# Two small loads on ScalarE's queue and the first token tile on the sync queue, in a one-layer hybrid attention kernel

## The chip, the core and the metric

The kernel runs on one core of one Trainium2 chip. The metric is device time in microseconds (us) of one execution; several executions are timed and the median is taken. Engines are named as in the profile: PE (TensorE; PEld its weight loads), DVE (VectorE), ACT (ScalarE), POOL (GpSimd), SP (the sync engine, which only issues transfers). A transfer can be issued by SP, ACT or POOL; the profile calls their queues SPq, ACTq and POOLq.

## The reference

One layer over 512 tokens of width 2048, float32: a norm, one wide projection, two groups of attention heads, gates, one output projection, a residual.

```python
h = rms_norm(x, norm_g)                      # x 512 x 2048, norm_g 2048
proj = h @ w_in                              # 2048 x 8192: qA kA vA gA | qB kB vB gB, 1024 columns each
ya = stick_breaking_attention(qA, kA, vA)    # 8 heads of 128, strictly causal
yb = chunk_band_attention(qB, kB, vB, q_norm_g, k_norm_g, rel_bias)   # 8 heads, band of 9 chunks of 64
mixed = concat(ya * silu(gA), yb * silu(gB))
out = x + mixed @ w_out                      # 2048 x 2048
```

The factor `norm_g` is applied to the channels of x before the projection; the division by the root mean square is per token and is applied later, to results.

## The kernel before

All products are float32, made of float32r halves: a tile is split into a high part (a copy to float32r, on ACT) and a low part (the difference, on DVE), and a product is three matmuls (high by high, high by low, low by high). Most of the projection goes through Winograd's seven products for a 2 x 2 block matrix. Output columns come in 32 units of 256, and the contraction of 2048 channels in steps.

The token side: the 16 channel blocks of x (128 channels x 512 tokens, 256 KB each, `xT[:, j, :]`) are paired, block j with block j + 8. `activations(j, 0)` loads a pair into one tile of four quarters of 256 columns: its `first` transfer (L687) fills quarters 0 and 3 with block j, its `second` (L688) fills quarters 1 and 2 with block j + 8. Pair 0 and pair 1 lie in the tile `xq`. `raw_split` then makes the high part on ACT with the channel's factor from `ng_t` as scale (L766), and the low part on DVE (L767); for quarter 3 of pair 0 the high part is made on DVE as well (L764).

The weight side: the weights of steps 0 and 1 (`n` below 2, the first two units, rows of the first two pairs) come in eight pieces of 128 KB, `load(n, i, kk)` (L384). `split` makes their high parts on ACT (L454) and their low parts on DVE (L458). The first product of the program needs piece (0, 0, 0), the `first` half of pair 0 and `ng_t`. The first two units use wide products only: each is one matmul at L773 and two at L775, of 512 columns. Eight matmuls on zeros (L1573) run ahead of them.

`ng_t` is a tile of 128 x 16 (64 bytes per partition, 8 KB), the whole of `norm_g`. In the kernel before it is loaded by POOL, with `pool.dma_start(ng_t, ng)` (L130), ahead of POOL's constants (L1574 to L1578). ACT issues one transfer in all, the `first` of pair 0, ahead of loading its function table (L1582). Every other load of this part is issued by SP.

What sets the order on each engine is a planner inside the kernel. Generators (`step_weights`, `activations`, `split`, and so on) yield operations `Op(engine, cost, fn, due)`; the planner keeps a clock of its own, and on each engine takes the operation with the earliest due time among those that are ready. `need(k, before)` is a due time: the moment at which product k begins by the planner's table, less `before`. So a different queue or due time at the start can also change, by a few rows, what the planner does later. A transfer's landing is told by one of eight semaphores for ACT's and SP's queues together (`DMAHW0` to `DMAHW7` in the listings below), given out in turn; the ninth transfer waits until the one that had its semaphore has landed. POOL's transfers have others (`DMASW`).

After the statistics of x (`x_stats`, `x_rstd`), DVE makes four diagonal blocks (L1233) and PE multiplies them by ones (L1240), which spreads the tokens' factors over the partitions. This stands where the Winograd products of the later units (L846 and L848) begin.

Of the kernel before, what the change touches and what calls it, by code (L numbers as in the profile page):

```python
# [15 lines left out]
P = 128  # L16
# [14 lines left out]
H = 256  # L31
# [43 lines left out]
def trunk_kernel(ctx: ExitStack, tc: tile.TileContext, xT, xn, wi, wqk, wo, ng, qg, kg, rel, out):  # L75
# [29 lines left out]
    act, dve, pe, sp, pool = nc.scalar, nc.vector, nc.tensor, nc.sync, nc.gpsimd  # L105

    def single(shape, name, dt=F32):
        return cp.tile(shape, dt, tag=name, name=name)

    def tmp(shape, tag, name, dt=F32, bufs=1):  # L110
        return wp.tile(shape, dt, tag=tag, name=name, bufs=bufs)

    ident = single([P, P], "ident")
    ng_t = single([P, NK], "ng_t")
# [12 lines left out]
    halves = banks.rearrange("p a (b c) -> p (a b) c", c=H)  # L127
    mixd = [dp.tile([P, S], F32, tag=f"mixd{i}", name=f"mixd{i}") for i in range(2 * NG)]

    pool.dma_start(ng_t, ng)  # L130

    KB = 256
    arena = single([P, 28 * KB], "arena")
# [8 lines left out]
    def avail(r):  # L142

        return all(r[1] <= x[0] or x[1] <= r[0] for x in taken.values())

    def claim(key, r):
        assert avail(r), (key, r, taken)
        taken[key] = r
        return arena[:, r[0]:r[1]] if r[0] < 100 * KB else parts[:, r[0] - 100 * KB:r[1] - 100 * KB]
# [39 lines left out]
    def AC(w, fn, due=None, n=1):  # L189
        return Op("ACT", (0.085 + 0.85e-3 * w) * n, fn, due)  # L190
# [14 lines left out]
    def advance(gen, rank):  # L205
        r = next(gen, None)
        if r is None:
            return
        if isinstance(r, Op):

            wait = 0.06 if r.engine != "PE" else 1.4 if position[0] < at_step[step_of[NU-4, 0]] else 0.6
            later(clock[0] + wait, lambda: ready[r.engine].append((r, gen, rank, count[0])))
        else:
            waiting.append((rank, r, gen))

    def spawn(gen, rank=(0,)):
        advance(gen, rank)
# [60 lines left out]
    def chunk(u):  # L278
        g, kind = u // 4, u % 4
        return (16 if g % 2 else 0) + kind * 4 + g // 2  # L280
# [4 lines left out]
    def rows(n):  # L285


        u, r = steps_[n]
        if u < NU:
            return (wi[chunk(u), h + r // 2, :, r % 2 * 2:r % 2 * 2 + 2, :] for h in (0, 2))  # L290
        q, i, h = u - NU, r // 2, r % 2
        return (wo[2 * i + k, q, :, h, :].rearrange("p (a b) -> p a b", b=H) for k in (1, 0))
# [9 lines left out]
    def plain(u, r):  # L302
        return u < 2 or u == NU and r < PLAIN_STEPS
# [67 lines left out]
    def need(k, before=0.0):  # L371

        return lambda: clock[0] + begins[k] - begins[position[0]] - before

    wt_, whl, at_end = {}, {}, {}

    def wt_place(n):
        return WT[olds.index(n) % 3]

    def load(n, i, kk=None):  # L380
        if n not in wt_:
            wt_[n] = claim(("wt", n), wt_place(n))
        x = slice(0, 2) if kk is None else slice(kk, kk + 1)
        sp.dma_start(wt_[n][:, 2 * i * H:2 * (i + 1) * H].rearrange("p (a b) -> p a b", b=H)[:, x, :], list(rows(n))[i][:, x, :])  # L384
        if i and kk != 0:
            done.add(("loading", n))

# [5 lines left out]
    def step_weights(n):  # L393
        i_ = olds.index(n)
        yield lambda: n < 2 or ("loading", olds[i_ - 1]) in done
        if n > before_major[-1]:
            yield lambda: ("taken", NM - 1) in done
        yield lambda: avail(wt_place(n))
        k = at_part[n, 0]
        if n < 2:  # L400

            for kk in range(2):
                for i in range(2):
                    k_ = k + 2 * i + 2 * len(BOTH) * kk
                    yield Op("SP", 0.47, lambda: load(n, i, kk), need(k_, 8), lag=P * 1024, quick=True)
                    spawn(landed_half(n, k_, i, kk), (0, n, i))
            return

        def both():
            for i in range(2):  # L410
                load(n, i)

        yield Op("SP", 0.94, both, need(k, 11 if n < 2 * NR else 7), lag=P * 4096)
        if plain(*steps_[n]):
            yield from split(n, 0, k)
        else:
            yield from sums(n, k, at_part[n, 1])

    def landed_half(n, k, i, kk):
        at_ = dma_free[0] + LANDING  # L420
        later(at_, lambda: None)
        yield lambda: clock[0] >= at_ - 1e-9
        yield from split(n, 0, k, i, kk)
# [11 lines left out]
    def split(n, part, k, piece=None, kk=None):  # L435

        w = (8 * P, 6 * P)[part]
        c = slice(0, w) if piece is None else slice(piece * w // 2, (piece + 1) * w // 2)
        if kk is not None:
            c = slice(c.start + kk * H, c.start + (kk + 1) * H)  # L440
        t = wt_[n][:, part * 8 * P + c.start:part * 8 * P + c.stop]
        i = having[part].index(n)
        yield lambda: i < 1 or ("hi", having[part][i - 1], part) in done
        yield lambda: n < before_major[-1] + 1 or ("hl", NP * NM - 1) in done
        homes = WHL[part] + ([(116 * KB, 124 * KB)] if n < 2 * NR else [])
        yield lambda: (n, part) in whl or any(avail(x) for x in homes)

        def hi():
            if (n, part) not in whl:
                r_ = next(x for x in homes if avail(x))  # L450
                whl[n, part] = claim(("w", n, part), r_).rearrange("p (a b) -> p a b", a=2)
                at_end.setdefault(last_use[n, part], []).append(("w", n, part))
                done.add(("hi", n, part))
            act.copy(whl[n, part][:, 0, c], t)  # L454

        yield AC(c.stop - c.start, hi, need(k, 2.6))
        h, l = whl[n, part][:, 0, :], whl[n, part][:, 1, :]
        yield DV(c.stop - c.start, lambda: dve.tensor_tensor(out=l[:, c], in0=t, in1=h[:, c].bitcast(F32), op=ALU.subtract),  # L458
                 need(k, 0.5))
        for x in (2,) if part else (0, 1) if piece is None else (piece,):  # L460
            done.add(("w", n, x) if kk is None else ("w", n, x, kk))
        if part or all(("w", n, x) in done or all(("w", n, x, y) in done for y in range(2)) for x in range(2)):
            done.add(("split", n, part))
            if ("split", n, 0) in done and (("split", n, 1) in done or (n, 1) not in at_part):
                unclaim(("wt", n))
# [187 lines left out]
    def activations(j, mixed):  # L653

        if mixed:
# [4 lines left out]
            k = at_step[step_of[NU, j]]  # L660
            kt, dt = at_step[step_of[NU + plain(NU, j), j]], 0
        else:
            k = at_step[step_of[0, j // 2]] + (2 * len(BOTH) if j == 1 else 0)
# [7 lines left out]
        if mixed:  # L671
            if HOME[j] == "qk" and "qk" not in staged:
                staged["qk"] = tmp([P, 2, 4 * H], "qk", "xm")
            r = staged["qk"][:, 0, :] if HOME[j] == "qk" else tmp([P, 4 * H], HOME[j], f"x{j}{mixed}")
        elif STAGE[j % 6] == "qk":
            if "x" not in staged:
                staged["x"] = tmp([P, 2, 4 * H], "qk", "xq")
            r = staged["x"][:, j % 2, :]
        else:
            r = tmp([P, 4 * H], STAGE[j % 6], f"x{j}")  # L680
# [2 lines left out]
        f = lambda x: x.rearrange("p a b -> p (a b)")  # L683
        a, b = (mixd[NJ + j], mixd[j]) if mixed else (xT[:, j, :], xT[:, j + NJ, :])

        queue, engine = (act, "ACT") if j == 0 and not mixed else (sp, "SP")
        first = lambda: queue.dma_start(r.rearrange("p (a b) -> p a b", b=H)[:, 0:4:3, :], a.rearrange("p (a b) -> p a b", b=H))  # L687
        second = lambda: sp.dma_start(r[:, H:3 * H], b)  # L688
        one = ("B11",), f(h[:, :1]), f(l[:, :1])
        spawn(raw(j, mixed, Op(engine, 0.47, first, need(k, 10 if mixed or j != 1 else 9), lag=P * 2048), r, k,  # L690
                  [(0, 1) + one] + ([(3, 4, ("B12",)) + ((f(h[:, 6:]), f(l[:, 6:])) if not mixed else (None, None))] if not mixed or plain(NU, j) else []), j, not mixed, kt, dt), (0, 0, j))
        spawn(raw(j, mixed, Op("SP", 0.47, second, need(k + 2 * mixed, 7.95 if engine == "ACT" else 9), lag=P * 2048), r, k + 2,
                  [(1, 3, ("B21", "B22"), f(h[:, 1:3]), f(l[:, 1:3]))], j + NJ, not mixed, kt, dt), (0, 0, j))
        yield lambda: all(("scaled", j, i, mixed) in done for i in (j, j + NJ))
        if mixed:
# [45 lines left out]
    def raw(j, mixed, load_, r, k, parts, channels, scaled, kt, dt):  # L741
        yield load_
        g_ = ng_t[:, channels:channels + 1] if scaled else None
        for x in parts:
            spawn(raw_split(j, mixed, r, k + 3 if mixed and x[2] == ("B12",) else k, g_, *x), (0, 0, j))
        if scaled and parts[-1][2] == ("B12",):

            yield lambda: ("x", j, "B12", 0) in done and position[0] >= START
            s_ = r[:, 3 * H:]
            yield AC(H, lambda: act.activation(s_, s_, AF.Copy, scale=g_), need(kt, 6 + dt))  # L750
        done.add(("scaled", j, channels, mixed))
# [41 lines left out]
    for k in reversed(range(len(program))):  # L793
        n, x, a = program[k]
        u = steps_[n][0]
        b = major_bank(*steps_[n]) if major(u) else place(u, a, x[2]) // 2
# [812 lines left out]
    for g in range(NG):  # L1609
        for h in range(2):  # L1610
            n = head(g, h)
# [52 lines left out]
```

## Time and profile before

| what | value |
|---|---|
| median of 3 runs | 906.84 us (906.5 to 908.52) |
| the profiled execution's own time | 908.72 us |
| its span, first to last instruction | 907.0 us, so 1.72 us lie outside it |
| PE busy | 898.4 us, 99% |
| DVE busy | 768.6 us, 85% |
| ACT busy | 636.8 us, 70% |
| POOL busy | 67.9 us, 7% |
| transfers on ACT's queue | 1, of 256 KB, 3.7 us from issue to landing |
| load of `ng_t` on POOL's queue | 8 KB, 4.1 us from issue to landing |

In a timeline row stand the start, the time from there to the end of the last instruction of the row, the engine, the line, the operation and its count; in brackets the engine's idle time before it and what ended that. In a row of transfers stand the queue, the count, the size of one and the median time from issue to landing. A row of windows has the stretch, its length, and for each engine its busy time and instructions, then the granted clock, the busy share of the transfer engines and GB/s.

### The profile page before, as it was taken

To read this page: it belongs to the slowest core of one execution; us is meant where nothing else is said; L and a number is where in the kernel's file an instruction comes from. 1 tells how busy PE (TensorE), PEld (TensorE's weight loads), DVE (VectorE), ACT (ScalarE), POOL (GpSimd) and SP (SyncE) were. 2 spreads that over 40 slices of the span, in tenths; PEclk is the share of its full clock that TensorE was granted. 3 is DMA by queue.
4 is the path that set the end of the run, shared out by engine and by line. 5 is a ranking of instruction groups with operands and counts; after the bars stand their busy time and mean duration, and the time that the engine had idled before them with its cause. 6 is when DMAs were issued, how large, how long until landed. Compare 5 with 4: busy or idle time off the path is not lost.

```text
span 907.0 us, 15445 instructions
## 1 busy us (share of the span) xinstructions
PE 898.4 (99%) x5504; PEld 802.1 (88%) x5504; DVE 768.6 (85%) x1255; ACT 636.8 (70%) x1203; POOL 67.9 (7%) x92
## 2 busy tenths in 40 slices
PE   8999999999999999999999999999999999999997
PEld 6898888888888888888888888888888988999997
DVE  6999989788898878788979787889878988988786
ACT  7785967697688658885877588868767885544342
POOL 0001100010000010000000100010000000101011
PEclk9999999999999999999999999999999999999999
DMA  8767677767666877677768775776665536657371
GB/s 303 247 202 170 155 171 182 183 154 177 172 164 154 198 184 168 157 174 184 166 151 207 182 168 142 184 192 159 151 163 126 186 116 206 159 197 190 114 186 47
DMA packets 187725, 156.22 MB, mean 172 GB/s; under 512 B 8944, under 2 KB 157440, under 8 KB 187648
## 3 DMA queue, kind: packets, MB, share of 16 engines
q1 hardware_dynamic: 177552, 122.45, 44.9%
q0 software_dynamic: 9824, 32.52, 22.0%
q8 instruction: 43, 0.70, 0.3%
q14 instruction: 34, 0.28, 0.1%
q10 hardware_dynamic: 272, 0.26, 0.1%
HBM read 117.45 MB, written 8.39 MB: 139 GB/s over the span
## 4 chain that ended last, share of the span: by engine, by line
PE 95%; DMA 2%; DVE 1%; ACT 1%; issue 0%; SPq 0%; DVEq 0%; POOLq 0%
PE banks L846 39%; PE banks L775 20%; PE banks L848 19%; PE banks L773 10%; PE banks L1479 2%; PE banks L836 2%; DMA arena<-in_wi 1%; PE banks L1385 1%; PE banks L837 1%; PE banks L1502 1%; DMA ng_t<-in_ng 0%; DVE parts L576 0%; ACT parts L575 0%; PE banks L1311 0%; DVE co L1074 0%
## 5 line engine op out<-in xcount | busy, mean ns | idle before, releaser
L846 PE MATMUL banks<-x,parts 128*128 128x512 f32 x1568 | 501.2, 401 | 0.0
L848 PEld LDWEIGHTS banks<-x,parts 128*128 128x128 f32 x1568 | 294.3, 188 | 70.1 <-DVE parts L576 0.7
L848 PE MATMUL banks<-x,parts 128*128 128x256 f32 x1568 | 309.8, 279 | 0.0
L576 DVE TENSOR_TENSOR parts<-arena,parts 128x1024 fp32r<-128x1024 f32 x196 | 239.1, 1221 | 66.7 <-ACT parts L575 66.3
L575 ACT CAST parts<-arena 128x1024 fp32r<-128x1024 f32 x196 | 205.8, 1051 | 110.7 <-PE banks L846 82.2
L846 PEld LDWEIGHTS banks<-x,parts 128*128 128x128 f32 x1568 | 240.5, 189 | 0.9
L775 PE MATMUL banks<-parts,x 128*128 128x256 f32 (+1 forms) x672 | 134.6, 298 | 0.0
L454 ACT CAST parts<-arena 128x1024 fp32r<-128x1024 f32 (+2 forms) x86 | 77.2, 909 | 72.1 <-PE banks L775 38.6
L775 PEld LDWEIGHTS banks<-parts,x 128*128 128x128 f32 x672 | 107.5, 191 | 3.7
L458 DVE TENSOR_TENSOR parts<-arena,parts 128x1024 fp32r<-128x1024 f32 (+2 forms) x86 | 89.2, 1047 | 15.4 <-ACT parts L454 15.2
L773 PE MATMUL banks<-parts,x 128*128 128x256 f32 (+1 forms) x336 | 100.4, 299 | 0.0
L775 PE MATMUL banks<-x,parts 128*128 128x256 f32 (+1 forms) x320 | 75.7, 329 | 0.2 <-DVE parts L458 0.2
L544 DVE TENSOR_TENSOR arena<-arena 128x1024 f32<-128x1024 f32 x56 | 68.3, 1219 | 5.6 <-DMA arena<-in_wi 4.8
L773 PEld LDWEIGHTS banks<-parts,x 128*128 128x128 f32 x336 | 63.9, 190 | 3.2
L775 PEld LDWEIGHTS banks<-x,parts 128*128 128x128 f32 x320 | 54.4, 192 | 5.9 <-DVE parts L458 0.7
L773 PE MATMUL banks<-x,parts 128*128 128x256 f32 (+1 forms) x160 | 53.4, 334 | 1.0 <-ACT parts L454 1.0
L536 POOL DMA_DIRECT2D arena<-arena x28 | 24.4, 870 | 331.3 <-DVE arena L544 73.8
L613 DVE TENSOR_TENSOR arena<-banks,arena 128x512 f32<-128x512 f32 x56 | 38.3, 684 | 6.4 <-PE banks L848 4.3
L555 POOL DMA_DIRECT2D arena<-arena x28 | 24.3, 869 | 216.5 <-DVE parts L576 149.6
L773 PEld LDWEIGHTS banks<-x,parts 128*128 128x128 f32 x160 | 30.8, 192 | 4.6 <-ACT parts L454 1.8
L628 DVE TENSOR_TENSOR c<-arena 128x1024 f32<-128x1024 f32 x28 | 34.1, 1219 | 0.5
L1488 DVE TENSOR_TENSOR wtl<-banks,wth 128x128 fp32r<-128x128 f32 (+1 forms) x64 | 31.0, 485 | 3.6 <-ACT wth L1487 3.4
(208 smaller groups left out, 1158.2 us busy)
## 6 DMA issues: line engine op xcount, KB each, us to landing
arena<-in_wi SPq DMA_DIRECT2D x308, 256.0 KB, 4.4
arena<-arena POOLq DMA_DIRECT2D x56, 512.0 KB, 5.5
arena<-in_wo SPq DMA_DIRECT2D x64, 256.0 KB, 3.1
xs<-in_xn SPq DMA_DIRECT2D x16, 256.0 KB, 4.7
mixd<-c SPq DMA_DIRECT2D x16, 256.0 KB, 3.8
out<-co SPq DMA_DIRECT2D x16, 256.0 KB, 4.7
x<-mixd SPq DMA_DIRECT2D x12, 256.0 KB, 4.4
co<-in_xn POOLq DMA_DIRECT2D x12, 256.0 KB, 6.9
```

What stands on the lines that cost most here:

```text
L454: act.copy(whl[n, part][:, 0, c], t)
L458: yield DV(c.stop - c.start, lambda: dve.tensor_tensor(out=l[:, c], in0=t, in1=h[:, c].bitcast(F32), op=ALU.subtract), need(k, 0.5))
L544: add = lambda x, due: DV(1024, lambda: dve.tensor_tensor(out=r("A21"), in0=r("A21"), in1=r(x), op=ALU.add), due)
L575: yield AC(1024, lambda: act.copy(v[:, 0, :], t), need(k, AHEAD[3]))
L576: yield DV(1024, lambda: dve.tensor_tensor(out=v[:, 1, :], in0=t, in1=v[:, 0, :].bitcast(F32), op=ALU.subtract), need(k, AHEAD[4]))
L613: join = lambda i, x, y, op=ALU.subtract: lambda: dve.tensor_tensor(out=c[:, i, :], in0=x, in1=y, op=op)
L628: yield DV(1024, lambda: dve.tensor_tensor(out=t_, in0=c[:, :, :H], in1=c[:, :, H:], op=ALU.add), clock[0] + 1.5)
L773: pe.matmul(o, lh, rh, start=start, stop=False, **kw)
L775: pe.matmul(o, x, y, start=False, stop=stop and (x is ll) != early, **kw)
L846: pe.matmul(both, mats[n][:, 0, j, :], X[j][:, :, i, :], start=p in (0, 1, 5) and j == 0, stop=False, skip_group_check=True)
L848: pe.matmul(o[:, :H], mats[n][:, 1, j, :], X[j][:, 0, i, :], start=False, stop=j == NJ - 1, skip_group_check=True)
L1488: yield DV(w, lambda: dve.tensor_tensor(out=tl[:, blocks, :], in0=tv, in1=th[:, blocks, :].bitcast(F32), op=ALU.subtract))
```

## The change

`ng_t` is loaded by ACT's queue instead of POOL's. The first piece of weights, (0, 0, 0), goes from SP's queue to ACT's. The `first` transfer of pair 0 goes from ACT's queue to SP's, and the due time of its `second` changes from 7.95 ahead of the product to 6.5.

```diff
-    pool.dma_start(ng_t, ng)
+    act.dma_start(ng_t, ng)
...
-    def load(n, i, kk=None):
+    def load(n, i, kk=None, queue=sp):
...
-        sp.dma_start(wt_[n][:, 2 * i * H:2 * (i + 1) * H].rearrange("p (a b) -> p a b", b=H)[:, x, :], list(rows(n))[i][:, x, :])
+        queue.dma_start(wt_[n][:, 2 * i * H:2 * (i + 1) * H].rearrange("p (a b) -> p a b", b=H)[:, x, :], list(rows(n))[i][:, x, :])
...
-                    yield Op("SP", 0.47, lambda: load(n, i, kk), need(k_, 8), lag=P * 1024, quick=True)
+                    queue, engine = (act, "ACT") if (n, i, kk) == (0, 0, 0) else (sp, "SP")
+                    yield Op(engine, 0.47, lambda: load(n, i, kk, queue), need(k_, 8), lag=P * 1024, quick=True)
...
-        queue, engine = (act, "ACT") if j == 0 and not mixed else (sp, "SP")
-        first = lambda: queue.dma_start(r.rearrange("p (a b) -> p a b", b=H)[:, 0:4:3, :], a.rearrange("p (a b) -> p a b", b=H))
+        first = lambda: sp.dma_start(r.rearrange("p (a b) -> p a b", b=H)[:, 0:4:3, :], a.rearrange("p (a b) -> p a b", b=H))
...
-        spawn(raw(j, mixed, Op("SP", 0.47, second, need(k + 2 * mixed, 7.95 if engine == "ACT" else 9), lag=P * 2048), r, k + 2,
+        spawn(raw(j, mixed, Op("SP", 0.47, second, need(k + 2 * mixed, 9 if mixed or j else 6.5), lag=P * 2048), r, k + 2,
```

From L384 to about L685 a line of the changed kernel has a number one higher than the same line before (L454 becomes L455). In the listings a name's last number is a tile's serial number.

ACT, from its first instruction, before:

```order
L687 DMA xq_123<-in_xT 128x2x256
L1582 ACT_TABLE_LOAD
L766 ACTIVATE x0_124<-xq_123,ng_t_69 128x256 [waits DMAHW0_49,DMASW0_49]
L454 CAST parts_100<-arena_99 128x256 [waits DMAHW1_49]
L766 ACTIVATE x0_124<-xq_123,ng_t_69 128x512 [waits DMAHW2_49]
```

And now:

```order
L130 DMA ng_t_69<-in_ng 128x16
L384 DMA arena_99<-in_wi 128x256
L1582 ACT_TABLE_LOAD
L766 ACTIVATE x0_124<-xq_123,ng_t_69 128x256 [waits DMAHW1_49,DMAHW0_49]
L455 CAST parts_100<-arena_99 128x256 [waits DMAHW2_49]
L766 ACTIVATE x0_124<-xq_123,ng_t_69 128x512 [waits DMAHW3_49]
```

ACT issues two transfers ahead of the table load instead of one, and `ng_t` has taken the first of the eight semaphores, so that all others stand one further.

SP, from its first instruction to the first waits for a semaphore's earlier transfer, before:

```order
L384 DMA arena_99<-in_wi 128x256
L688 DMA xq_123<-in_xT 128x512
L384 DMA arena_99<-in_wi 128x256 x2
L687 DMA xq_123<-in_xT 128x2x256
L384 DMA arena_99<-in_wi 128x256
L688 DMA xq_123<-in_xT 128x512
L384 DMA arena_99<-in_wi 128x256 [waits DMAHW0_49]
L384 DMA arena_99<-in_wi 128x256 [waits DMAHW1_49]
```

And now:

```order
L687 DMA xq_123<-in_xT 128x2x256
L688 DMA xq_123<-in_xT 128x512
L384 DMA arena_99<-in_wi 128x256 x2
L687 DMA xq_123<-in_xT 128x2x256
L384 DMA arena_99<-in_wi 128x256
L688 DMA xq_123<-in_xT 128x512 [waits DMAHW0_49]
L384 DMA arena_99<-in_wi 128x256 [waits DMAHW1_49]
L384 DMA arena_99<-in_wi 128x256 [waits DMAHW2_49]
```

SP's first row is the token tile instead of the piece of weights. The `second` of pair 1 now waits for `DMAHW0`, the landing of `ng_t`; the two rows behind it wait for the same two transfers as before (the `first` of pair 0, and piece (0, 0, 0)).

On POOL the row of L130 is gone and nothing stands in its place. Up to the statistics of x no other row of PE moves; on ACT, DVE and SP some rows trade places from about 20 us on. PE, where the statistics' product stands among the first Winograd products, before:

```order
L775 MATMUL banks<-x_308,parts 128x256 x2
L846 MATMUL banks<-x_124,parts 128x512
L846 MATMUL banks<-x_125,parts 128x512
L848 MATMUL banks<-x_124,parts 128x256
L848 MATMUL banks<-x_125,parts 128x256
L1240 MATMUL banks<-diag,ones 128x128 x4
L846 MATMUL banks<-x_145,parts 128x512
```

And now:

```order
L775 MATMUL banks<-x_306,parts 128x256 x2
L1240 MATMUL banks<-diag,ones 128x128 x4
L846 MATMUL banks<-x_124,parts 128x512
L846 MATMUL banks<-x_125,parts 128x512
L848 MATMUL banks<-x_124,parts 128x256
L848 MATMUL banks<-x_125,parts 128x256
L846 MATMUL banks<-x_143,parts 128x512
```

The product of the diagonals stands four matmuls earlier on PE. DVE, which makes the diagonals, before:

```order
L544 TENSOR_TENSOR arena<-arena 128x1024
L1233 TENSOR_SCALAR diag<-ident,rstd 128x128 x3
L1005 TENSOR_TENSOR c_778<-banks,arena 128x256
L1233 TENSOR_SCALAR diag<-ident,rstd 128x128
L1008 TENSOR_TENSOR c_778<-banks,c_778 128x256
```

And now:

```order
L545 TENSOR_TENSOR arena<-arena 128x1024
L1233 TENSOR_SCALAR diag<-ident,rstd 128x128 x4
L1005 TENSOR_TENSOR c_779<-banks,arena 128x256
L1008 TENSOR_TENSOR c_779<-banks,c_779 128x256
L577 TENSOR_TENSOR parts<-arena,parts 128x1024
```

One operation (L1005) has moved from ahead of the fourth diagonal to behind it. From some 116 us into the span on, the order of all engines is the same as before.

More of the change, by code (lines that the diff above doesn't have):

```diff
@@ L684, in activations @@
         a, b = (mixd[NJ + j], mixd[j]) if mixed else (xT[:, j, :], xT[:, j + NJ, :])
-        queue, engine = (act, "ACT") if j == 0 and not mixed else (sp, "SP")
-        first = lambda: queue.dma_start(r.rearrange("p (a b) -> p a b", b=H)[:, 0:4:3, :], a.rearrange("p (a b) -> p a b", b=H))
+        first = lambda: sp.dma_start(r.rearrange("p (a b) -> p a b", b=H)[:, 0:4:3, :], a.rearrange("p (a b) -> p a b", b=H))
         second = lambda: sp.dma_start(r[:, H:3 * H], b)
         one = ("B11",), f(h[:, :1]), f(l[:, :1])
-        spawn(raw(j, mixed, Op(engine, 0.47, first, need(k, 10 if mixed or j != 1 else 9), lag=P * 2048), r, k,
+        spawn(raw(j, mixed, Op("SP", 0.47, first, need(k, 10 if mixed or j != 1 else 9), lag=P * 2048), r, k,
                   [(0, 1) + one] + ([(3, 4, ("B12",)) + ((f(h[:, 6:]), f(l[:, 6:])) if not mixed else (None, None))] if not mixed or plain(NU, j) else []), j, not mixed, kt, dt), (0, 0, j))
-        spawn(raw(j, mixed, Op("SP", 0.47, second, need(k + 2 * mixed, 7.95 if engine == "ACT" else 9), lag=P * 2048), r, k + 2,
+        spawn(raw(j, mixed, Op("SP", 0.47, second, need(k + 2 * mixed, 9 if mixed or j else 6.5), lag=P * 2048), r, k + 2,
                   [(1, 3, ("B21", "B22"), f(h[:, 1:3]), f(l[:, 1:3]))], j + NJ, not mixed, kt, dt), (0, 0, j))
```

## The prediction

> **What bounds the kernel now.** I read the page first, for the engine that fills the span.
>
> ```profile
> span 907.0 us, 15445 instructions
> PE 898.4 (99%) x5504; PEld 802.1 (88%) x5504; DVE 768.6 (85%) x1255; ACT 636.8 (70%) x1203; POOL 67.9 (7%) x92
> PE 95%; DMA 2%; DVE 1%; ACT 1%; issue 0%; SPq 0%; DVEq 0%; POOLq 0%
> ```
>
> PE is busy for 99% of the span and makes up 95% of the chain that ended last. So an edit at the start counts by how much earlier PE begins its real products, provided that nothing later gives it back. Next, the chain in order of time over the first 20 us (start, length, what).
>
> ```profile
> 1.29 4.11 DMA ng_t<-in_ng
> 5.40 0.02 issue
> 5.43 0.52 ACT x L766
> ...
> 7.24 1.22 PE banks L775 x2
> ```
>
> The start hangs on one transfer: POOL issues `ng_t` at 1.29 and it lands at 5.40; ACT starts 0.03 later. The timeline shows the other loads, and PE's wait.
>
> ```profile
> 0.75 0.46 ACTq L687 DMA_DIRECT2D xq<-in_xT  x1
> 0.75 0.39 SPq L384 DMA_DIRECT2D arena<-in_wi  x1
> 1.20 0.42 SPq L688 DMA_DIRECT2D xq<-in_xT  x1
> 1.24 1.28 ACT L1582 ACT_TABLE_LOAD   x1 [1.24 <-PEq L1656]
> 1.47 3.78 PE L1573 MATMUL banks<-parts 128*128 128x512 f32 x8 [1.47 <-DVE parts L1571]
> 3.59 0.43 SPq L688 DMA_DIRECT2D xq<-in_xT  x1
> 4.49 2.76 SPq L384 DMA_DIRECT2D arena<-in_wi  x6
> 5.43 0.51 ACT L766 ACTIVATE x<-xq,ng_t 128x256 fp32r<-128x256 f32 x1 [2.90 <-DMA ng_t<-in_ng]
> 5.84 0.39 ACT L454 CAST parts<-arena 128x256 fp32r<-128x256 f32 x1
> 6.13 0.72 ACT L766 ACTIVATE x<-xq,ng_t 128x512 fp32r<-128x512 f32 x1
> 6.28 0.80 PE L773 MATMUL banks<-x,parts 128*128 128x512 f32 x1 [1.03 <-ACT parts L454]
> 7.24 1.22 PE L775 MATMUL banks<-x,parts 128*128 128x512 f32 x2 [0.16 <-DVE parts L458]
> ```
>
> PE runs the eight matmuls on zeros until 5.25, then idles 1.03 us. The transfers, issue to landing (the last field), come from the view of transfers in short windows.
>
> ```profile
> arena<-in_wi SPq DMA_DIRECT2D x1, 128.0 KB, 3.0
> xq<-in_xT ACTq DMA_DIRECT2D x1, 256.0 KB, 3.7
> xq<-in_xT SPq DMA_DIRECT2D x1, 256.0 KB, 4.0
> ng_t<-in_ng POOLq DMA_DIRECT2D x1, 8.0 KB, 4.1
> qg_t<-in_qg SPq DMA_DIRECT2D x1, 0.5 KB, 5.7
> ```
>
> So the first piece of weights is there at 0.75 + 3.0 = 3.75, the `first` half of pair 0 at 0.75 + 3.7 = 4.45, its `second` at 1.20 + 4.0 = 5.20, and `ng_t` alone keeps ACT until 5.40.
>
> **The change, part by part.** *`ng_t` to ACT's queue.* It is ACT's first instruction, at 0.75. The trace has no 8 KB load on this queue. From below: the load issued at the same moment with idle transfer engines, 128 KB in 3.0, gives 3.75. From above: its own 4.1 gives 4.85, and the 0.5 KB `qg_t`, issued later among full queues, 5.7, gives 6.45. I take 3.0, since that row shares the moment and the idle engines, and 8 KB is less than 128.
>
> ```profile
> 0.00:1.50 1.50, 0.03 (x1) 0.04 (x1) 0.48 (x1) 0.26 (x1) 0.42 (x5) 1.00 0.00 0
> 1.50:2.00 0.50, 0.50 (x1) 0.47 (x2) 0.00 (x0) 0.50 (x1) 0.50 (x2) 1.00 0.15 18
> 4.50:5.00 0.50, 0.50 (x2) 0.02 (x1) 0.00 (x0) 0.00 (x0) 0.00 (x0) 1.00 1.12 363
> ```
>
> These windows show why: the last two fields are the transfer engines' busy share and GB/s, 0.15 and 18 before 2.00, full at 363 when POOL's load still had not landed. As a check, the Trainium skill, page "DMA: Bandwidth & Descriptors", section "Latency and other measured facts", gives a first byte after some 0.6 us for SP's and ACT's queues and some 1 us for POOL's; by it `ng_t` would gain 0.54 of issue and 0.4 of start, an estimate of 4.46, which would make the sum below 0.94. No run here shows a first byte.
>
> *The token tile to SP's queue.* Issued at 0.75 as before, now by SP, with its `second` behind it instead of the weights. Bounds 3.0 (SP's first row) and 4.0 (SP's 256 KB row); I take its own 3.7, since bytes and moment are the same: 4.45. It becomes the last arrival, so ACT's L766 starts at 4.48, 0.95 earlier.
>
> *The first piece of weights to ACT's queue.* Behind `ng_t`, at 1.24, where the table load starts now. With 3.0 to 4.0 it lands between 4.24 and 5.24; L454 wants it at 5.84 - 0.95 = 4.89. Up to 3.65 it is hidden behind L766; at 4.0 it costs 0.35. I take it as hidden, since its one row says 3.0.
>
> *ACT's table load* moves back by one issue, some 0.46, to end near 3.0. ACT's idle 2.90 us ahead of L766 covers it; without that cover it would cost 0.46.
>
> *POOL* loses one instruction; nothing waits for its constants here: nothing.
>
> *The `second` half* stands behind 256 KB instead of 128 in SP's queue: some 0.35 us later at 363 GB/s, at 5.55 against a wish of 6.13 - 0.95 = 5.18. The products that read it are the third and fourth, seven matmuls on, and the stall of 0.37 lies beside them.
>
> *A new wait.* The eight semaphores make the `second` of pair 1 on SP (at 3.59 before) wait for `ng_t`. At 3.75 that costs 0.16 in SP's queue, ahead of six loads of weights which already wait:
>
> ```profile
> SPq L384 <- DMA xq<-in_xT: 0.6, 2, 0.5
> ```
>
> The first of these issued at 4.49, when the token tile had landed (4.45); it waits for the same transfer still. So 0.16 vanishes there.
>
> *Sum.* The first product from 6.28 to 5.33, just behind the zeros' end at 5.25; DVE's part of it depends on the same landing, so the second matmul moves from 7.24 to 6.29. Gain 0.95 us, with bounds 0.55 (`ng_t` at 4.85) and 1.65 (both at 3.75: the first product then waits for the zeros, and the weights' low part for the piece at 4.24, second matmul at 5.59).
>
> *Does it last?* Later work would have to move too.
>
> ```profile
> 46.41 1.05 ACT L454 CAST parts<-arena 128x1024 fp32r<-128x1024 f32 x1 [1.26 <-PE banks L775]
> 47.49 1.23 DVE L458 TENSOR_TENSOR parts<-arena,parts 128x1024 fp32r<-128x1024 f32 x1 [0.89 <-ACT parts L454]
> 48.00:56.00 8.00, 8.00 (x53) 7.31 (x52) 8.00 (x13) 8.00 (x16) 0.00 (x0) 1.00 0.53 167
> 71.42 0.41 DVE L1005 TENSOR_TENSOR c<-banks,arena 128x256 f32<-128x256 f32 x1
> 71.75 0.27 DVE L1233 TENSOR_SCALAR diag<-ident,rstd 128x128 f32<-128x128 f32 x1
> 71.97 0.63 PE L846 MATMUL banks<-x,parts 128*128 128x512 f32 x2
> 72.67 1.05 PE L1240 MATMUL banks<-diag,ones 128*128 128x128 f32 x8
> ```
>
> ACT and DVE are paced by PE: the split of weights at 46.41 had waited for PE to release the space, so it moves along. The one place where the new order presses is the diagonals. They were done at 72.02, PE used them at 72.67: 0.65 spare. DVE makes the fourth 0.33 sooner now (71.75 - 71.42), PE asks 0.70 sooner (72.67 - 71.97). 0.28 remain if DVE moves along, so no stall; if it did not move at all, PE would stall for 0.95 - 0.28 = 0.67.
>
> **TensorE's speed.** Early matmuls are slower, for a reason that waits do not show:
>
> ```profile
> 8.26 0.63 PE L773 MATMUL banks<-x,parts 128*128 128x512 f32 x1
> 8.68 1.05 PE L775 MATMUL banks<-x,parts 128*128 128x512 f32 x2
> 10.37 0.39 PE L773 MATMUL banks<-x,parts 128*128 128x512 f32 x1
> 10.60 0.63 PE L775 MATMUL banks<-x,parts 128*128 128x512 f32 x2
> ```
>
> At 8.26 starts are 0.42 apart, at 10.37 0.23, with the granted clock at 1.00 in the windows: half speed until about 9.8. Eight steps lie between 7.24 and 10.37, so full speed from 7.24 on would save 3.13 - 8 x 0.23 = 1.29. The profiled execution took 908.72, the median is 906.84; I read the 1.88 between them as mostly this, an argument the runs' times alone allow. The Trainium skill, "TensorE: Matmul & The Clock Gate", Part 1, says that full speed follows a busy window of about 3.4 us that runs free of the kernel, so that the moment differs from run to run. The rows agree in the halving, and no row here shows the window.
>
> **How the numbers follow.** The profiled execution would go from 908.72 to 907.77; on the median, 906.84 - 0.95 = 905.89. A change of under 0.2%, 1.8 us, is about what measurement of this kernel can't tell from none.
>
> - Forecast, 0.50: the gain of 0.95, 905.9. Its own range 905.2 to 906.3 (gains 1.65 to 0.55).
> - Rival: full speed does not come along, 0.20. If its moment stays at 9.8 in the profiled state, the 0.95 are spent at half speed and yield 0.95 x 0.23 / 0.42 = 0.52. If most runs after are late where the median before was early, 905.89 + 1.29 to 1.88 is 907.2 to 907.8. For it: nothing in the change sets that moment. Against: PE's idle time ahead of the products shrinks from 1.03 to 0.08.
> - Rival: only the issue is saved, 0.10. `ng_t` keeps its 4.1 and lands at 4.85: gain 0.55, 906.3. Against it, the idle engines of the first windows. The Trainium skill, "DMA: Bandwidth & Descriptors", section "Issuing engines are not separate DMA queues", says just that: another queue saves only the sequencer's time.
> - Rival on the other side: a tiny load on ACT's queue is slow, 0.06. Like `qg_t`'s 5.7, `ng_t` lands at 6.45; products start 1.05 later, SP's loads behind the new wait 2.86 later (6.45 - 3.59). It decides once the load takes over 4.65 (5.40 - 0.75). Time 907.9.
> - Rival: given back at the diagonals, 0.07. Stall 0.67, gain 0.28, 906.6.
> - A larger gain, 0.07: the bound of 1.65 and a later wait of PE dissolved,
>
> ```profile
> 134.40 0.45 PE L773 MATMUL banks<-qk 128*128 128x384 f32 x1 [0.36 <-DVE c L1542]
> ```
>
> 0.36 more: 904.8.
>
> The range 905.0 to 907.9 leaves out the last case and the worst of the late ones, under 2 in 10. Faster than 905.03: the last case and the edge of the forecast, 0.11. Slower than 908.65 needs the slow load together with late full speed, 0.05. The rest, 0.84, is within 0.2%.
>
> **What would show it.** Right: `ng_t` landing by 4; ACT's wait ahead of its first L766 ended by the token tile instead of `ng_t`, near 4.5; PE's first L773 near 5.3 with an idle time near 0.1; no idle PE at L1240 near 71. Wrong: `ng_t` landing past 4.85; ACT's first L454 waiting for weights; starts 0.42 apart past 9.8; DVE's L1233 ending PE's wait; a new idle time of over 0.5 us on PE between 20 and 140 us.

## The result, and the profile after

The changed kernel takes 905.33 us in the median (904.75 to 905.84, 10 runs), the kernel before 906.68 beside it (906.41 to 908.52, 10 runs). The ratio of the runs is 0.9981, with a 95% interval of 0.9972 to 0.9989 (the quotient of the two medians alone is 0.9985). So it is faster, by 1.35 us in the medians, and the interval does not reach 1. The two sets of runs do not overlap. The prediction had 905.9, and took a change of under 0.2% for one that can't be told from none.

The profiled execution took 905.52 us, 0.19 above the median; that of before, at 908.72, stood 2.04 above its own. The two profiles are therefore 3.2 us apart and the medians only 1.35, a difference that the experiments below explain.

First the page: span, engines, and the chain that ended last.

```profile
span 903.7 us, 15445 instructions
PE 896.9 (99%) x5504; PEld 801.2 (89%) x5504; DVE 768.9 (85%) x1255; ACT 637.9 (71%) x1203; POOL 66.4 (7%) x91
PE 97%; DMA 1%; ACT 1%; DVE 1%; issue 0%; SPq 0%; DVEq 0%; ACTq 0%
```

PE's share of the chain has gone from 95% to 97%, that of transfers from 2% to 1%. The chain in order of time (start, length, what) names another load at the start:

```profile
0.75 0.42 ACTq L130
...
1.20 3.54 DMA arena<-in_wi
...
5.23 0.50 PE banks L773
```

`ng_t` is only there as the instruction that the first piece of weights had to be issued behind. That piece lands at 4.74 and is now what PE waits for. The timeline of the same stretch:

```profile
1.47 3.69 PE L1573 MATMUL banks<-parts 128*128 128x512 f32 x8 [1.47 <-DVE parts L1571]
3.96 0.51 ACT L766 ACTIVATE x<-xq,ng_t 128x256 fp32r<-128x256 f32 x1 [0.99 <-DMA xq<-in_xT]
4.50 0.88 DVE L767 SCALAR_TENSOR_TENSOR x<-xq,ng_t,x 128x256 fp32r<-128x256 f32 x2 [0.16 <-ACT x L766]
4.77 0.41 ACT L455 CAST parts<-arena 128x256 fp32r<-128x256 f32 x1 [0.31 <-DMA arena<-in_wi]
5.23 0.50 PE L773 MATMUL banks<-x,parts 128*128 128x512 f32 x1
5.29 0.42 DVE L459 TENSOR_TENSOR parts<-arena,parts 128x256 fp32r<-128x256 f32 x1
5.77 0.74 PE L775 MATMUL banks<-x,parts 128*128 128x512 f32 x2
6.35 0.40 PE L773 MATMUL banks<-x,parts 128*128 128x512 f32 x1
6.58 0.63 PE L775 MATMUL banks<-x,parts 128*128 128x512 f32 x2
...
7.75 0.39 PE L773 MATMUL banks<-x,parts 128*128 128x512 f32 x1
```

Four things are to be seen. The zeros end at 5.16 and the first product starts at 5.23: PE's idle time of 1.03 us is gone. ACT's L766 starts at 3.96, released by the token tile. The second matmul follows 0.54 behind the first instead of 0.96, since DVE has done the token side's low parts (L767) while it waited for the weights. And the starts are 0.23 apart from 6.35 on, where the profile of before had 0.42 until about 9.8. Full speed had come sooner still: the eight zeros take 3.69 us instead of 3.78, and the first product 0.50 instead of 0.80. Each trace also keeps a record of the granted clock, with the moment at which it rises to full speed: 4.91 us here, 9.81 in the profile of before.

The transfers (queue, count, size, us from issue to landing):

```profile
xq<-in_xT SPq DMA_DIRECT2D x1, 256.0 KB, 3.1
ng_t<-in_ng ACTq DMA_DIRECT2D x1, 8.0 KB, 2.4
arena<-in_wi ACTq DMA_DIRECT2D x1, 128.0 KB, 3.5
```

Later on, the matmuls of the diagonals and the place near 134 us, then all that PE still waits for (total, times, longest):

```profile
69.34 1.06 PE L1240 MATMUL banks<-diag,ones 128*128 128x128 f32 x8
131.51 0.44 PE L773 MATMUL banks<-qk 128*128 128x384 f32 x1
PE banks L1573 <- DVE parts L1571: 1.5, 1, 1.5
PE banks L1479 <- ACT W L1464: 0.3, 1, 0.3
```

No bracket stands behind L1240, nor behind the L773 that waited 0.36 us for L1542 before.

Between the two profiles the spans differ by 3.2 us. The second matmul starts 7.24 - 5.77 = 1.47 earlier. The tenth product matmul starts 10.37 - 7.75 = 2.62 earlier, so half speed accounts for 1.15 more. The wait near 134 us adds 0.36. The remaining 0.2 lies behind 627 us, where a wait for L1488 comes and goes from run to run with either order.

### The profile page after: what moved, and what is told of

It reads as the page before. It is cut to its first block, busy times and chain, and to the rows that moved or that the text cites. A ratio compares the mean times of both kernels' runs of the same rounds, so it can differ in the third digit from the quotient of the medians.

```text
span 903.7 us, 15445 instructions
## 1 busy us (share of the span) xinstructions
PE 896.9 (99%) x5504; PEld 801.2 (89%) x5504; DVE 768.9 (85%) x1255; ACT 637.9 (71%) x1203; POOL 66.4 (7%) x91
## 4 chain that ended last, share of the span: by engine, by line
PE 97%; DMA 1%; ACT 1%; DVE 1%; issue 0%; SPq 0%; DVEq 0%; ACTq 0%
PE banks L846 39%; PE banks L775 21%; PE banks L848 20%; PE banks L773 10%; PE banks L1479 2%; PE banks L836 2%; PE banks L1385 1%; DMA arena<-in_wi 1%; PE banks L837 1%; PE banks L1502 1%; ACT parts L576 0%; PE banks L1311 0%; DVE co L1074 0%; ACT W L1455 0%; DVE parts L577 0%
## 5 line engine op out<-in xcount | busy, mean ns | idle before, releaser
L455 ACT CAST parts<-arena 128x1024 fp32r<-128x1024 f32 (+2 forms) x86 | 77.3, 909 | 69.3 <-PE banks L775 33.1
L773 PE MATMUL banks<-parts,x 128*128 128x256 f32 (+1 forms) x336 | 100.3, 299 | 0.0
L773 PEld LDWEIGHTS banks<-parts,x 128*128 128x128 f32 x336 | 63.9, 190 | 3.2
L773 PE MATMUL banks<-x,parts 128*128 128x256 f32 (+1 forms) x160 | 52.7, 330 | 0.1
L1488 DVE TENSOR_TENSOR wtl<-banks,wth 128x128 fp32r<-128x128 f32 (+1 forms) x64 | 30.9, 483 | 3.6 <-ACT wth L1487 3.4
L773 PEld LDWEIGHTS banks<-x,parts 128*128 128x128 f32 x160 | 30.4, 190 | 3.5 <-ACT parts L455 0.7
```

What stands on the lines that cost most here:

```text
L773: pe.matmul(o, lh, rh, start=start, stop=False, **kw)
L1488: yield DV(w, lambda: dve.tensor_tensor(out=tl[:, blocks, :], in0=tv, in1=th[:, blocks, :].bitcast(F32), op=ALU.subtract))
```

## The experiments

The theory that they test has three terms. The products start earlier, by 1.0 to 1.5 us. Full speed, which comes after a stretch of PE work without much idle time, is no longer delayed by the gap ahead of the first product. And the planner's new order takes away the wait near 134 us. The rivals: one of the two edits does it alone; or full speed is luck of the run and owes nothing to the change. The experiments ran in three sets, the first two on one chip and the third on another; the kernel before took 908.46 us there (35 runs), 908.32 (25) and 908.29 (23), longer than in the first comparison. The 83 runs lie in groups: 18 from 906.63 to 907.20, 58 from 907.52 to 909.21, 7 from 909.37 to 910.72. Why more of them are late than in the first comparison is open.

### Only `ng_t` moved

```diff
-    pool.dma_start(ng_t, ng)
+    act.dma_start(ng_t, ng)
```

> Theory (the start: what lands last, and an unbroken start of PE): norm_g on ACT's queue lands by 3.2 as in the changed kernel, but the token tile is now ACT's second transfer, issued near 1.20, and lands near 4.7 (3.5 for that); L766 near 4.7, first product near 5.6, second near 6.5, PE idle 0.4 us between the zeros and the first product. The order of all engines is that of before. Time 905.7 to 906.0, no run near 908. Rival (the gain is the order that the planner changed later, or transfers' contention): about 906.5 with runs near 908.2 as before.

Measured: 908.85 us (906.84 to 910.54, 12 runs), ratio 1.0006 (0.9995 to 1.0016): nothing gained. The transfers, ACT's wait and PE's:

```profile
xq<-in_xT ACTq DMA_DIRECT2D x1, 256.0 KB, 4.0
ng_t<-in_ng ACTq DMA_DIRECT2D x1, 8.0 KB, 2.5
5.30 0.51 ACT L766 ACTIVATE x<-xq,ng_t 128x256 fp32r<-128x256 f32 x1 [2.34 <-DMA xq<-in_xT]
6.15 0.79 PE L773 MATMUL banks<-x,parts 128*128 128x512 f32 x1 [0.90 <-ACT parts L454]
134.96 0.44 PE L773 MATMUL banks<-qk 128*128 128x384 f32 x1 [0.53 <-DVE c L1542]
```

`ng_t` lands near 3.25, but the token tile, pushed to ACT's second place (issued at 1.19), takes 4.0 and lands at 5.2. One late load has been exchanged for another, 0.2 us earlier. I had expected a gain here; that was a miss.

### Only the queues of the tile and the piece swapped

```diff
-    act.dma_start(ng_t, ng)
+    pool.dma_start(ng_t, ng)
```

(against the changed kernel, whose order on all engines stays.)

> norm_g on POOL's queue, the rest of the change kept, so the order of all engines is that of the changed kernel. Theory: norm_g still lands near 5.4 and keeps ACT until then; first product near 6.28; PE idle 1.0 us ahead of it; times split as before, some near 906.5 and some near 908.2, less at most 0.7 if the later waits of PE (0.36 at 134 us, 0.38 at 634 us) are gone by the order alone. Rival (the order carries the gain): about 905.3, no run near 908.

Measured: 908.22 us (906.11 to 909.35, 12 runs), ratio 0.9995 (0.9985 to 1.0004).

```profile
ng_t<-in_ng POOLq DMA_DIRECT2D x1, 8.0 KB, 4.2
6.37 0.80 PE L773 MATMUL banks<-x,parts 128*128 128x512 f32 x1 [1.12 <-ACT parts L455]
134.56 0.44 PE L773 MATMUL banks<-qk 128*128 128x384 f32 x1
```

The start is as late as before, and half speed lasted until about 10.7. The wait near 134 us is gone although `ng_t` is as late as before: it goes with the order that the planner makes after the swap, not with `ng_t`. The same holds in all profiles: the six with the order of before have this wait, 0.36 to 0.53 us, and the eight with the changed order have none. Neither edit alone can be told from no change; the start needs both.

### Fewer zeros in the changed kernel

```diff
-WARM = 8
+WARM = 5
```

> The changed kernel with 5 matmuls on zeros instead of 8; they end near 3.9, so PE idles some 1.3 us ahead of the first product, which stays at 5.23. Theory: full speed is late again in a good part of the runs or in all, these near 906.6 to 907.5, with starts 0.42 apart until 8 us or later. Rival: 905.3, as the changed kernel.

Measured: 906.94 us (906.25 to 907.67, 11 runs), ratio to before 0.9984 (0.9975 to 0.9992). The changed kernel took 905.39 on the same chip, in the second set (below).

```profile
1.47 2.50 PE L1573 MATMUL banks<-parts 128*128 128x512 f32 x5 [1.47 <-DVE parts L1571]
5.24 0.79 PE L773 MATMUL banks<-x,parts 128*128 128x512 f32 x1 [1.27 <-DVE x L767]
5.83 1.09 PE L775 MATMUL banks<-x,parts 128*128 128x512 f32 x2
...
8.43 1.05 PE L775 MATMUL banks<-x,parts 128*128 128x512 f32 x2
...
9.65 0.63 PE L775 MATMUL banks<-x,parts 128*128 128x512 f32 x2
```

The products start at the same moments as in the changed kernel (5.24 and 5.83 against 5.23 and 5.77), and the order is the same. Only the gap of 1.27 us is back, and with it half speed until about 9.6. That costs 906.94 - 905.39 = 1.55 us (0.8 to 2.5 by resampling the runs). So the gap sets a part of the time that no wait of PE shows.

### More zeros in the kernel before: ten, then fourteen

```diff
-WARM = 8
+WARM = 10
```

> The kernel before with 10 matmuls on zeros instead of 8; they end near 6.1, so PE idles 0.2 instead of 1.0 us ahead of the first product, which stays at 6.28. Theory (the idle time on PE makes full speed come late in some runs): no run near 908.2, all near 906.5, matmul starts 0.23 apart from the second product matmul on. Rival (full speed comes late by chance, whatever the gap, or the slow runs have another cause): about 4 in 10 runs near 908.2 as before.

Measured with ten: 907.88 us (906.76 to 910.98, 12 runs), ratio 0.9997 (0.9986 to 1.0009). Half of the runs stay at 908.1 or above, a miss. In its profile, an early run at 906.81, PE is busy until the first product, but a hole is left between the first and the second:

```profile
6.11 0.80 PE L773 MATMUL banks<-x,parts 128*128 128x512 f32 x1
7.07 0.73 PE L775 MATMUL banks<-x,parts 128*128 128x512 f32 x2 [0.16 <-DVE parts L458]
```

The starts are 0.96 apart where a half-speed matmul takes 0.43, so half a microsecond is idle (the 0.16 counts from an end that is modelled). Fourteen zeros, at half speed, cover that too.

> The kernel before with 14 matmuls on zeros: PE has no gap from 1.47 on, and its first product follows the zeros, at 6.3 (full speed early) to 7.5 (late), instead of 6.28; so PE starts its products up to 1.2 us later. Theory: all the same no run comes late by a stretch: runs within 1.5 us of each other, 906.4 to 907.9, none above 908.2, median below that of before on this chip. Rival (the wide times have another cause than PE's gap): spread as before, up to 910, and 0 to 1.2 us slower.

Measured with fourteen: 907.0 us (906.44 to 908.07, 11 runs), ratio 0.9989 (0.9980 to 0.9998). In the third set, on the other chip:

> The kernel before with 14 zeros matmuls again, on the same chip as the other runs of this call. Theory: 906.8 to 907.2 as before, first product near 6.1, second near 7.0, a wait of 0.36 to 0.42 for L1542 near 133 us.

906.94 us (906.51 to 907.6, 11 runs), ratio 0.9987 (0.9978 to 0.9995). Two profiles, one of each:

```profile
1.47 4.82 PE L1573 MATMUL banks<-parts 128*128 128x512 f32 x14 [1.47 <-DVE parts L1571]
7.00 0.74 PE L775 MATMUL banks<-x,parts 128*128 128x512 f32 x2 [0.46 <-DVE parts L458]
...
132.98 0.44 PE L773 MATMUL banks<-qk 128*128 128x384 f32 x1 [0.42 <-DVE c L1542]
```

```profile
1.47 5.81 PE L1573 MATMUL banks<-parts 128*128 128x512 f32 x14 [1.47 <-DVE parts L1571]
7.11 0.40 PE L773 MATMUL banks<-x,parts 128*128 128x512 f32 x1
7.35 0.62 PE L775 MATMUL banks<-x,parts 128*128 128x512 f32 x2
```

In the one, full speed came during the zeros (at 4.36 by the clock record) and the idle time stands behind it; in the other the zeros, at half speed for longer (until 6.48), ran into the products and there was no idle time. The products start no earlier than before, the wait near 134 us is still there (0.42 and 0.40), and nothing but work on zeros was added. Yet the kernel is 1.3 us faster, and all 22 runs lie between 906.44 and 908.07, around the lowest group of before. So a gap ahead of full speed delays it, and the two lower groups of before's times are most likely told apart by that moment. The four profiles taken from the middle group, two of before and one of each edit alone, have it between 9.73 and 10.74, and that of the early run with ten zeros at 7.04; no run of before from the lowest or the highest group was profiled.

### The order alone, without the gap

This is the swap alone (second experiment) with fourteen zeros. Against before with fourteen, the queues of the tile and the piece and the planner's order differ.

```diff
-WARM = 8
+WARM = 14
```

> The queue swap alone (ng_t on POOL's queue, planner's order of the changed kernel) with 14 zeros matmuls in place of 8. Against before with 14 zeros it differs in the planner's order and the swapped queues alone; its products wait for the same late ng_t. Theory (the wait of PE near 134 us is worth its 0.4 us to the end): no idle of PE near 134; median 906.4 to 906.8, that is 0.2 to 0.6 under the kernel before with 14 zeros (907.0), and no run above 908. Rival (what is won there is given back to a later wait): 906.9 to 907.1, the same as the other.

Measured: 906.4 us (906.05 to 907.23, 11 runs), ratio to before 0.9982 (0.9973 to 0.9991). PE near 133 us, and at its one later wait for L1488:

```profile
132.93 0.44 PE L773 MATMUL banks<-qk 128*128 128x384 f32 x1
...
632.47 0.50 PE L773 MATMUL banks<-wth,v 128*128 128x512 f32 x1 [0.32 <-DVE wtl L1488]
```

The median is 0.54 under that of before with fourteen zeros in the same set; by the means, 906.56 and 906.96, it is 0.40, with standard errors of 0.13 and 0.11. That is the size of the wait (0.40 in the profile of before with fourteen zeros). But the runs overlap: resampled, the difference of the medians goes from -0.25 to 0.91 us. And the one profile, of the longest of the eleven runs (907.23), shows what the rival named: it waits 0.32 for L1488 at 632.47, where the profile of before with fourteen zeros, at 906.94, has no wait. So the removal of the wait near 134 us is shown, and that it is worth its 0.4 us to the end is likely and not settled.

### The two loads of ACT in the other order

```diff
-    act.dma_start(ng_t, ng)
...
     def constants():
+        yield Op("ACT", 0.47, lambda: act.dma_start(ng_t, ng), -6.0)
         yield Op("ACT", 1.28, lambda: act.preload_act_table_set(TABLES), -5.0)
```

The piece of weights is now issued at 0.75 and `ng_t` at 1.20.

> The changed kernel with ACT's two transfers in the other order: the piece of weights at 0.75, norm_g at 1.20. Theory of the landing (POOL's way costs the time, not the moment of issue): norm_g issued at 1.20 lands within 2.9, near 4.0, as against 4.1 us for POOL's issue at 1.29. Rival (a page of the notes: only the issue is saved): it lands near 5.3. The piece lands near 3.5 and no longer stops L454; the second matmul stays near 5.77, since DVE's chain sets it; time within 0.3 us of the changed kernel.

Measured: 905.75 us (905.51 to 908.11, 8 runs), ratio 0.9976 (0.9966 to 0.9986).

```profile
arena<-in_wi ACTq DMA_DIRECT2D x1, 128.0 KB, 3.0
ng_t<-in_ng ACTq DMA_DIRECT2D x1, 8.0 KB, 3.3
4.57 0.51 ACT L765 ACTIVATE x<-xq,ng_t 128x256 fp32r<-128x256 f32 x1 [1.60 <-DMA ng_t<-in_ng]
6.38 0.72 PE L774 MATMUL banks<-x,parts 128*128 128x512 f32 x2 [0.45 <-DVE parts L458]
```

`ng_t` lands at 4.5 now and holds ACT. Its 3.3 us lies between what the theory (at most 2.9) and the rival (4.1) gave. So the queue counts, at nearly the same moment of issue (1.20 here, 1.29 on POOL's queue); and so does being second and 0.45 later on ACT's queue, which this run cannot take apart. It is one profile. The second matmul was expected to stay near 5.77 and is 0.6 later than in the changed kernel, but the time cannot be told from its 905.4. One of the eight runs took 908.11, 1.8 above all others. This order is no better.

### Ten zeros in the changed kernel

```diff
-WARM = 8
+WARM = 10
```

> The changed kernel with 10 zeros matmuls in place of 8, so that PE is busy until 5.6 to 6.0 and does not idle ahead of the first product even where the first piece of weights lands late (5.00 in one profile). Theory: the gap of 0.07 to 0.25 us that is left in the changed kernel costs nothing, and the two matmuls more push the first product back by 0.1 to 0.5: median 905.3 to 905.9, not faster than the changed kernel. Rival (the gap left still delays full speed in some runs): narrower and faster, 904.8 to 905.2.

Measured: 905.66 us (905.11 to 906.3, 6 runs), ratio 0.9969 (0.9958 to 0.9981); the changed kernel beside it 905.42. Closing the last gap brings nothing that can be measured. None of the kernels tried beats the changed one.

### The two kernels again, for the scale

> The changed kernel itself, on one chip with the others. Theory (full speed follows a stretch of some 3.4 us in which PE has hardly idled; the stretches begin at a random moment, so it comes by some 8.3 us where PE never idles from 1.47 on, and one or two stretches later where a gap breaks it): runs within 1.2 us of each other, the highest at least 2 us below the highest of before. Rival (the spread of before is a trait of the chip or of transfers): as wide as before's runs on this chip.

> The changed kernel, on the same chip as the other runs of this call: 905.2 to 905.6, runs between 904.7 and 906.3, against 908.0 to 908.5 of the kernel before.

> The kernel before itself, for its own spread and a second profile: ratio 1.000 within its interval. Theory: in the profile the matmul from which starts are 0.23 apart tells the time: each us of half speed after the second matmul costs some 0.46 us of the time.

The changed kernel: 905.39 us (904.85 to 906.2, 6 runs), ratio 0.9970 (0.9959 to 0.9982), and 905.42 (904.73 to 905.8, 6 runs), ratio 0.9967 (0.9954 to 0.9979). The kernel before, run as an experiment: 908.01 (906.65 to 908.95, 11 runs), ratio 0.9996 (0.9988 to 1.0005). In another execution of the changed kernel the piece of weights landed later, at 5.00:

```profile
5.50 0.79 PE L773 MATMUL banks<-x,parts 128*128 128x512 f32 x1 [0.25 <-ACT parts L455]
6.98 0.56 PE L773 MATMUL banks<-x,parts 128*128 128x512 f32 x1
7.37 0.63 PE L775 MATMUL banks<-x,parts 128*128 128x512 f32 x2
```

PE idles 0.25 us and full speed comes near 7.3. That run took 906.2, the longest of the 12.

In the third set the three terms can be read on one chip: from 908.29 (before) to 906.94 with the gap covered, to 906.40 with the swap and its order as well, to 905.42 with the changed kernel, where `ng_t` is early and the zeros are eight again. That is 1.35 for full speed (0.5 to 1.9 by resampling the runs), 0.54 for the order (-0.25 to 0.91, so not clear of nothing) and 0.98 for the start (0.4 to 2.0), 2.87 in all.

How much idle time delays full speed can be read from the clock records of the 14 profiles. From the rise to the fall behind the last matmul it is, in each, 262 or 263 times 3.413 us, so the clock changes on a grid of that step. Count as idle what is left of a step when each matmul ahead of the rise gets 0.43 us, or less where the next starts sooner; the time ahead of the first zero is idle too. The step that ends with the rise then has at most 0.70 us of idle time in all 14 profiles, and the step before it, which did not bring full speed, at least 1.08. In the profile of before these are 0.69 and 1.23, and the second holds the gap of 1.03. So a gap costs a whole step of half speed when it takes the step over a limit that lies, by these profiles, between 0.70 and 1.08 us; and where the grid stands against the kernel's start differs from run to run. With ten zeros in the kernel before, the two holes come to 0.74 us, between the two bounds; its late runs were not profiled.

## Why the prediction was right and wrong

**The bound and the place were right.** One load held the start, `ng_t` landed by 4 us, ACT's first L766 is released by the token tile, and PE's idle time ahead of the first product is 0.07. In the profile all of the gain but the wait near 134 us and 0.2 behind 627 us is made by the tenth product.

**The token tile was mis-sized.** I gave it its old 3.7 us on SP's queue, landing at 4.45; it took 3.1 and landed at 3.85. `ng_t` landed at 3.15, for 3.75 in the sum. So L766 started at 3.96, not 4.48.

**The first piece of weights became the last arrival.** I took it as hidden. At 3.5 us it stayed under the 3.65 that I had allowed, but with the tile early it ended ACT's wait (0.31). The first product came at 5.23, for 5.33 in the sum.

**The second matmul did not keep its distance.** The sum moved it by 0.95 along with the first, as if DVE's part still waited for the token side. With the weights last, DVE had the token side done by 5.38, and the second matmul moved by 1.47. My bound of 1.65 contained this case (second matmul at 5.59), as the edge of the forecast's own range; the sum went by 0.95 all the same. The measured 905.33 lies inside that range (905.2 to 906.3), but three terms put it there, where the sum had one.

**Full speed was weighed with the wrong sign; this is the step that failed.** I wrote that its moment might "not come along", with a loss of 1.29 to 1.88, and as evidence against it that PE's idle time shrinks from 1.03 to 0.08. That same row should have been a gain. I had read the 1.88 us between before's profile and its median as half speed, rightly; from there a change that closes the gap gives that time back to each run that loses it. The sum had no such term and no case had it. The granted clock of 1.00 that I read beside the half-speed rows is no measurement either: the record of the clock begins with the rise, at 9.81, and the windows ahead of it show 1.00 for want of an entry. In the first comparison the term was partly hidden in the median: six of before's ten runs were early ones (906.41 to 906.84), four late (908.12 to 908.52). Against the early six alone (median 906.5) the gain is 1.2, so of the 1.35 some 0.2 is this term; by the means (907.23 and 905.34) the gain is 1.9, and 0.7 of it is this term. In the experiments most runs of before were late, and the gain is 2.9, of which fourteen zeros alone give 1.3. The 0.95 of the sum agrees with the 0.98 that the last step above gives for the start; how near they come is in part luck, since the landings and the second matmul were off in both directions.

**The wait near 134 us got too small a chance.** I priced it at 0.36, which its removal agrees with as far as the times can tell, and gave it 0.07 together with the largest start. It belongs to the planner's order, which is the same in every run, and the order can be listed ahead of the run; what the new order does to that wait could not be read from it alone.

**The diagonals** (0.07) did not stall: L1240 has no wait. **Only the issue saved** (0.10) is refuted for this load: from issue to landing `ng_t` took 2.0 to 2.7 us as ACT's first transfer and 3.8 to 4.4 on POOL's queue. The Trainium skill, page "DMA: Bandwidth & Descriptors", section "Issuing engines are not separate DMA queues", has another issuing engine save the sequencer's time alone; a difference of at least 1.1 us from issue to landing, in which the 0.54 of earlier issue is not counted, goes against it here. Part of that difference can come from the earlier moment: with `ng_t` second on ACT's queue, at 1.20, it is 0.5 to 1.1. The estimate of 4.46 for the landing was too late as well; it was 3.15. **A slow tiny load** did not come.

**The limit of 0.2%** was too wide as well, and it made the forecast one of no change that can be told. It stood on three runs of before, whose spread of 2 us is the moment of full speed, not the measurement. The changed kernel's ten runs spread over 1.1 us, and a difference of 1.35 could be told.

**What is not settled.** That a gap delays full speed is shown in both directions (zeros taken away and added). How long a gap must be is known only to the bounds above, 0.70 and 1.08 us of idle time in a step. The gap of 0.25 us in the changed kernel went with the latest of its three profiled moments, but there the step before the rise began at 0.48, ahead of the first zero at 1.47, and 0.99 of its 1.15 us of idle time lie there, not in the gap. The Trainium skill, "TensorE: Matmul & The Clock Gate", Part 1, puts it as a busy window of about 3.4 us that runs free of the kernel. By that rule, an estimate, PE busy from 1.47 on gets full speed between 4.9 and 8.3, and the three profiles of the changed kernel have it at 4.91, 6.03 and 7.31; starting anew at 5.24 with five zeros it comes between 8.6 and 12.0, and the profile has 9.57. Both agree, and so does the step of 3.413 us. One profile with fourteen zeros has 4.36, sooner than the estimate: its step began 0.5 us ahead of the first zero, so a step need not be busy throughout. Why `ng_t` needs over a microsecond less on ACT's queue than on POOL's was not taken apart further than into queue on the one hand, place and moment of issue on the other.

## What to carry to other kernels

Where the first work of TensorE runs below full speed, price an idle gap ahead of it twice: once as the wait, and once as the half-speed work that it prolongs. When the profiled execution stands far from the median, or the runs lie in groups, find out which moment differs before a change is judged by one execution. And when several loads meet in one instruction, move them together and ask which arrives last afterwards: here each move alone gave nothing, since another load or the same one still arrived at 5.2 to 5.5.

## What was not expected of the hardware

A gap of 1.27 us on PE, with the start of the products and the order unchanged, cost about 1.5 us, and the loss stands behind the wait that names it, as half speed until 9.57 instead of 4.91 to 7.31. In 14 profiles full speed came with the first step of a 3.413 us grid that had at most 0.70 us of idle PE time, and never with one that had 1.08 or more. A transfer of 8 KB took 2.0 to 2.7 us as ACT's first, 3.3 as ACT's second and 3.8 to 4.4 on POOL's queue. The 256 KB of the token tile took 3.5 to 3.7 as ACT's first and 4.0 as ACT's second; as SP's first they took 2.9 to 3.5 where `ng_t` went by ACT, but 3.8 and 4.0 where it went by POOL. Why is open.
